# Seven block products for the second half of the output gate and for the retention branch's gate, with their sums on VectorE and the convolution constants loaded row by row

## The chip, the cores and the metric

The kernel runs on one core of one Trainium2 chip. The metric is the device time of one execution in microseconds (us), lower is better. The engines are called as the profile calls them: PE (TensorE, matmuls), PEld (its weight loads), DVE (VectorE), ACT (ScalarE), POOL (GpSimd), SP (SyncE, which here only issues DMAs). L12 is line 12 of the kernel before.

## The reference, cut to what matters

One layer of a hybrid backbone on 128 context and 512 latent tokens, 640 rows in all, model width 1024. The normalised and modulated input `h` goes through one wide projection `w_in`; attention and retention use slices of it:

```python
z = h @ w_in
q, k, v, rq, rk, rv, rg, ga, gr = jnp.split(z, np.cumsum(IN_SPLITS)[:-1].tolist(), axis=-1)
...
o = rms_scale(o_f + o_b[:, :, ::-1])
o = o.transpose(0, 2, 1, 3).reshape(B, L, RET_V)
yr = jax.nn.silu(rg.astype(jnp.float32)) * o
...
y = jax.nn.sigmoid(ga) * (ya @ w_att_o) + jax.nn.sigmoid(gr) * (yr @ w_ret_o)
return y @ w_out
```

`rg` (1024 columns) is the output gate of retention, `gr` (1024 columns) the gate of the retention branch. After this come a gated residual, a second norm, a gated MLP with a width-3 convolution (constants `conv_w`, `conv_b`), and a final norm.

## The kernel before

**Precision.** Each matmul operand is split into a high part (a cast to the matmul type) and a low part (the rest), and each product is three matmuls: high by high, high by low, low by high. A helper `w_split` (L139) makes the parts of a weight: the high part by ACT (L147), the low part by DVE (L152), or, with `"dma"`, by a negated copy on ACT and an accumulating DMA issued by POOL. Raw weights come by `w_raw` (L136) into two buffers of 8 KB per partition (tag `raw`); parts lie in eight buffers of 1024 columns (tag `wh`).

**Two forms of projection.** `a_group` keeps 128 tokens stationary and streams 512 weight columns: five banks, twelve matmuls of 512 columns for each half of the contraction and each token tile, 120 in all (L159 to L161). `b_col` keeps 128 weight columns stationary and streams 320 tokens: two banks of 24 matmuls (L197 to L199).

**Seven products.** The output projection `w_ret_o` (`ret_unit`, L1114) already uses Winograd's form of Strassen's scheme. A unit is 256 output columns; contraction, tokens and columns are each cut in two, and instead of eight block products it makes seven (numbered 1, 5, 6, 2, 3, 7, 4), each of twelve matmuls of 320 columns, on sums of blocks. The sums of the activations are made once by `ret_sums` (L1076, in tiles `ys`), those of the weights for each unit by `wsum` (L1129). `prod` (L1169) issues a product and takes its bank into the outputs; `prep` (L1133) makes the parts of one weight block; `ret_pump` (L1219) runs `prep` ahead of the products as far as the `wh` buffers go.

**Order around the change.** After the value projection (`rv1`) `states` (L909) makes the chunk states `Ss`. `retention` (L1011) runs ten groups (five token tiles by two halves of the heads) in three steps: `ret_a` (transposed keys `rkT`), `ret_b` (scores, L980, masked by DVE at L982) and `ret_c` (L989, L991; the square sums go to `sso`). The scaled queries `qd` (four buffers) are moved by `ret_q` (L955) on SP's queue and scaled at L969. `conv_load` (L1005) waits for the first `rkT` by a copy on POOL (L1006) and then issues four DMAs of single elements, three of `conv_w` (L1008) and one of `conv_b` (L1009). `ret_d` (L998) normalises a half of the heads; its root is a chain of thirteen small DVE steps and a scaling (`rsqrt`, L210 to L222), followed by five multiplications (L1003). Between these run the blocks of `rg0`, the first half of the output gate, by `a_group`; `evac_rg` (L1035) applies tanh (L1038) and multiplies (L1039, L1041). Then come the second half, `evac_rg(1)`, by `a_group`; then eight columns of the branch gate by `b_col` in `gr_col` (L1103; tanh at L1105), with the transposes of the gated retention output (`yr_blocks`, L1062 to L1067, parts by L665 and L666) and `ret_sums` beside them; then the four units of `w_ret_o`.

Outside the blocks marked `manual_schedule` a planner orders the instructions of every engine, and it may issue loads well ahead of their place in the program; inside such a block the named engines keep the written order. The block that holds the branch gate and `w_ret_o` fixes PE, DVE and ACT.

## Time and profile before

| | |
|---|---|
| median of three runs | 1138.04 us (1137.78 to 1138.88) |
| the profiled execution | 1138.44 us |
| its span, first to last instruction | 1136.7 us |
| mean granted PE clock | 0.998 |
| instructions | 17580 |

The span is what the profile's rows cover; the 1.7 us between it and the execution's time lie outside them. In the views that follow, a group's row has the line, the engine, the operation, output and inputs, the shape and the count, then busy time and the mean length of one in ns, then the idle time of the engine just before it and what ended that. A row of the timeline starts with the start time and the length in us, with the wait before it in brackets at its end.

### The profile page before, as it was taken

The page shows a single profiled execution, that of the slowest core. Times are in us where ns is not written, and L with a number is a line of the kernel's source. Part 1 is how long each engine was busy: PE and PEld are TensorE (multiplying, and loading weights), DVE is VectorE, ACT ScalarE, POOL GpSimd, SP SyncE. Part 2 cuts the span into 40 slices and gives each one's busy share as a digit, 9 for nine tenths or more (in the row PEclk, how much of TensorE's full clock was granted, in tenths as well). Part 3 has the DMA queues.
Part 4 walks back from the last instruction along what each step waited for, and adds up shares of the span by engine and source line. Part 5 has one row for each costly group of instructions (what it writes and reads, how often), then busy time and mean ns, then how long its engine had stood idle before and what let it go on. Part 6 is the DMA issues. An engine that isn't in the chain of part 4 may idle for free.

```text
span 1136.7 us, 17580 instructions
## 1 busy us (share of the span) xinstructions
PE 1109.3 (98%) x6757; PEld 1009.6 (89%) x6757; DVE 844.2 (74%) x1456; ACT 594.5 (52%) x1120; POOL 142.9 (13%) x171
## 2 busy tenths in 40 slices
PE   5999999999999999999999999999999999999996
PEld 4788899999989878889999889999899899899995
DVE  4667877669959947565857648968687598589888
ACT  5355756554244234534336436677557466475473
POOL 0042200000000010000003032012111111121012
PEclk9999999999999999999999999999999999999999
DMA  9742111016945734611228937456657646576552
GB/s 307 246 152 74 39 37 38 2 37 215 323 146 174 243 115 110 78 38 38 74 72 163 302 132 212 130 112 121 143 139 158 157 80 167 130 128 155 136 130 93
DMA packets 139316, 151.99 MB, mean 134 GB/s; under 512 B 27976, under 2 KB 108952, under 8 KB 138976
## 3 DMA queue, kind: packets, MB, share of 16 engines
q1 hardware_dynamic: 109856, 119.65, 33.3%
q0 software_dynamic: 29104, 31.10, 17.2%
q8 instruction: 53, 0.87, 0.3%
q14 instruction: 31, 0.25, 0.1%
q10 hardware_dynamic: 272, 0.11, 0.0%
HBM read 115.71 MB, written 8.67 MB: 109 GB/s over the span
## 4 chain that ended last, share of the span: by engine, by line
PE 88%; DVE 5%; ACT 3%; issue 2%; DMA 1%; SPq 0%; ACTq 0%; DVEq 0%; POOL 0%
DMA weights.raw.247_7726<-in_w_down 1%; DVE x1.u1.1_6330 L1496 1%; DMA ret2.qd.12_4681<-ret.u5.5_3422 0%; DMA const.u2.2_72<-in_b_mod 0%; DVE x1.u1.1_6330 L1545 0%; DVE x1.u1.1_6330 L1303 0%; PE mm3.mm.75_6171 L1176 0%; DVE acts.u2.2_91 L432 0%; PE mm1.mm.11_294 L161 0%; PE mm7.mm.59_10668 L1619 0%; PE mm7.mm.17_8071 L1619 0%; PE mm7.mm.41_9543 L1619 0%; PE mm7.mm.59_10668 L1618 0%; PE mm7.mm.44_9776 L1618 0%; PE mm7.mm.38_9294 L1619 0%
## 5 line engine op out<-in xcount | busy, mean ns | idle before, releaser
L1148 POOL DMA_DIRECT2D weights.wh.164_5865<-weights.raw.156_5798 x1 | 1.3, 1327 | 146.9 <-DVE f1.s.15_5209 L1187 146.9
L816 POOL DMA_DIRECT2D spill.u2.2_2891<-f1.s.1_1160 x1 | 0.6, 580 | 129.7 <-DVE mod.u3.3_2846 L604 129.7
L1633 DVE TENSOR_TENSOR t7.u4.4_6818<-t7.u4.4_6818,const.u1.1_70 128x320 f32<-128x320 f32 x10 | 4.9, 494 | 11.4 <-ACT const.u1.1_70 L1632 11.4
L152 DVE TENSOR_TENSOR weights.wh.113_4453<-weights.raw.111_4450,weights.wh.112_4452 128x1024 fp32r<-128x1024 f32 x1 | 1.2, 1227 | 13.1 <-ACT weights.wh.112_4452 L147 13.1
L938 DVE SCALAR_TENSOR_TENSOR ret2.u1.1_4263<-ret2.u1.1_4263,const.u11.11_86 64x128 f32<-64x128 f32 x24 | 6.8, 338 | 2.9 <-ACT ret2.u1.1_4263 L931 2.8
L940 DVE SCALAR_TENSOR_TENSOR ret2.u1.1_4263<-ret2.u1.1_4263,const.u11.11_86 64x128 f32<-64x128 f32 x24 | 6.6, 382 | 2.8 <-ACT ret2.u1.1_4263 L933 2.8
L429 ACT CAST acts.u1.1_90<-f0.s.2_104 128x640 fp32r<-128x640 f32 x4 | 2.9, 728 | 9.5 <-DVE f0.s.2_104 L427 9.5
L553 ACT ACTIVATE f0.s.3_710<-f0.s.3_710,p1q.ny20.11_878 128x128 f32<-128x128 f32 x20 | 6.0, 388 | 2.5 <-DVE p1q.ny20.11_878 L220 2.5
L446 PE MATMUL aux1.aux.1_134<-const.u1.1_70,const.u2.2_72 80*128 80x80 f32 x1 | 0.4, 367 | 7.1 <-DMA const.u2.2_72<-in_b_mod 7.1
L429 ACT CAST acts.u1.1_90<-f0.s.1_103 128x640 fp32r<-128x640 f32 x4 | 2.9, 727 | 8.3 <-DVE f0.s.1_103 L427 8.3
L299 POOL DMA_DIRECT2D mod.acc.24_3630<-in_b_mod x2 | 1.7, 858 | 42.5 <-ACT ret.u5.5_3422 L874 42.5
L147 ACT CAST weights.wh.67_3284<-weights.raw.66_3282 128x1024 fp32r<-128x1024 f32 x1 | 1.1, 1052 | 11.3 <-PE mm3.mm.8_3125 L198 11.3
L147 ACT CAST weights.wh.77_3520<-weights.raw.76_3518 128x1024 fp32r<-128x1024 f32 x1 | 1.0, 1048 | 11.2 <-PE mm3.mm.16_3382 L198 11.2
L584 POOL TENSOR_TENSOR p1.u1.1_604<-p1.u3.3_608,p1q.u1.1_598 128x512 f32<-128x512 f32 x1 | 1.3, 1302 | 44.5 <-DMA p1.u4.4_610<-in_cache_k 44.5
L1150 DVE TENSOR_TENSOR weights.wh.152_5717<-weights.raw.151_5663,weights.wh.152_5717 128x512 fp32r<-128x512 f32 x1 | 0.7, 693 | 8.3 <-ACT weights.wh.152_5717 L1141 8.3
L147 ACT CAST weights.wh.132_5219<-weights.raw.131_5217 128x1024 fp32r<-128x1024 f32 x1 | 1.1, 1055 | 11.0 <-PE mm3.mm.49_5037 L160 11.0
L1507 DVE TENSOR_TENSOR x1.u1.1_6330<-x1.u1.1_6330,gate.u1.1_6316 128x512 f32<-128x512 f32 x10 | 6.7, 693 | 0.0
L553 ACT ACTIVATE p1.u4.4_610<-p1.u4.4_610,p1.ny10.15_660 128x128 f32<-128x128 f32 x10 | 3.0, 389 | 6.5 <-DVE p1.ny10.15_660 L220 6.5
L1540 POOL TENSOR_TENSOR x1.u1.1_6330<-x1.u1.1_6330,weights.raw.422_10889 128x512 f32<-128x512 f32 x3 | 4.9, 1632 | 12.2 <-ACT x1.tm.111_10902 L1513 9.4
L446 PEld LDWEIGHTS aux1.aux.1_134<-const.u1.1_70,const.u2.2_72 80*128 80x128 f32 x1 | 0.2, 182 | 7.0 <-issue 7.0
L152 DVE TENSOR_TENSOR weights.wh.83_3656<-weights.raw.81_3653,weights.wh.82_3655 128x1024 fp32r<-128x1024 f32 x1 | 1.2, 1226 | 6.9 <-ACT weights.wh.82_3655 L147 6.9
L553 ACT ACTIVATE f0.s.4_959<-f0.s.4_959,p1q.ny20.20_1127 128x128 f32<-128x128 f32 x20 | 6.2, 396 | 0.0
(6808 smaller groups left out, 4938.1 us busy)
## 6 DMA issues: line engine op xcount, KB each, us to landing
spill.u1.1_2890<-x1.u1.1_6330 POOLq DMA_DIRECT2D x5, 512.0 KB, 3.9
xin.u1.1_102<-in_x_sample SPq DMA_DIRECT2D x4, 512.0 KB, 4.6
p0.u5.5_119<-in_w_mod SPq DMA_DIRECT2D x2, 1024.0 KB, 10.0
p0.u6.6_125<-in_w_mod SPq DMA_DIRECT2D x2, 1024.0 KB, 14.9
p0.u7.7_128<-in_w_mod SPq DMA_DIRECT2D x2, 1024.0 KB, 12.3
...
```

The source lines that it names most:

```text
L147: nc.scalar.copy(hi, rv)
L152: (lo_eng or V).tensor_sub(lo, rv, hi.bitcast(F32))
L299: nc.gpsimd.dma_start(accs[v][0:1, c, :], a["b_mod"][0:1, col:col + DM], accum_op=ALU.add)
L429: nc.scalar.copy(hT[0][:, k, :], xk)
L553: nc.scalar.activation(x[:, j], x[:, j], AF.Copy, scale=rstd[:, j:j + 1])
L584: nc.gpsimd.tensor_mul(ct, r2[:, :, 0, :], gqk[:, i:i + 1, :].to_broadcast([P, 4, P]))
L938: V.scalar_tensor_tensor(Ss[0:64, hh, st + 1, j], Ss[0:64, hh, st, j], cdsel[0:64, h:h + 1], Ss[0:64, hh, st + 1, j], op0=ALU.mult, op1=AL ...
L940: V.scalar_tensor_tensor(Ss[64:128, hh, 2 - st, j], Ss[64:128, hh, 3 - st, j], cdsel[64:128, h:h + 1], Ss[64:128, hh, 2 - st, j], op0=ALU. ...
L1496: V.tensor_add(x1[:, t, gs], x1[:, t, gs], down_mul(ps, t, c0))
L1507: V.tensor_mul(x1[:, t, gs], x1[:, t, gs], gb[:, t == 0, gs])
L1540: eng.tensor_mul(x, x, fg[:, c0:c0 + 512])
L1633: V.tensor_sub(his[1], his[1], u3[i])
```

## The change

Both gates are moved to the seven-product form, as six units of 256 columns ahead of the four units of `w_ret_o`, all in one list of products with one `ret_pump`.

- `h_sums` makes the four sums of blocks of `h` on DVE, in pieces of 640 columns, between the steps of `states` and of `retention`. Its running sum `x` borrows one of the two `raw` buffers; the fourth sum goes to the space of `Ss` for the first half of the heads and is made late.
- `in_unit` prepares weight blocks as `ret_unit` does, but the low parts of products 2, 3 and 7 go by accumulating DMA, and the high part of 7 by a copy on DVE. `rg_col` and `gr_col` apply tanh afterwards, in place, from SBUF.
- The low parts of `rg0` go by DMA.
- The second half of the heads is normalised, transposed and gated inside the list (`plan`): the transposes of that half are multiplied by the gate straight from PSUM, and the low parts and sums of the retention output are spread over the products.
- `ret_d` takes its root from one power on POOL and one refinement on DVE.
- `conv_load` loads one row at a time, at groups 2, 4, 6 and 8, each after a copy on POOL that waits for the keys of the group before.
- `r2k` has five buffers, not six; `r1` and `crow` lie in other pools; pool `f1` closes early and `hs` takes its place.

```diff
     def r2k():
-        return rp([P, 512], tag="r2k", bufs=6)
-
-    r1 = rp([P, NT, 2, 64])
+        return rp([P, 512], tag="r2k", bufs=5)
+
+    r1 = modp([P, NT, 2, 64])
...
+    def h_sums():
+        q = {m: [z.bitcast(F32) for z in hq[m]] for m in hq}
+        x = wp([P, 4 * 512], F32, tag="raw", bufs=2)[:, :4 * HALF].rearrange("p (k t) -> p k t", k=4)
...
+        yield from diff(x, q[1, 1], q[1, 0])
+        yield from low(1)
+        yield from neg_sum(x, q[0, 0])
+        yield from low(2)
+        yield from diff(h3, q[0, 0], q[1, 0])
+        yield "late"
+        yield from neg_sum(h4, q[0, 1])
...
     def ret_d(hh):
-        rso = rsqrt(rs2, sso[:, hh].rearrange("p t h -> p (t h)"), 4 * NT, 1.0 / P, post=0.5)
+        rso = sso[:, hh].rearrange("p t h -> p (t h)")
+        y = cv[:, 4:7, :].rearrange("p r c -> p (r c)")[:, :4 * NT]
+        V.tensor_scalar(rso, rso, 1.0 / P, EPS, op0=ALU.mult, op1=ALU.add)
+        nc.gpsimd.tensor_tensor(y, rso, cst[:, C_NH:C_NH + 1].to_broadcast([P, 4 * NT]), op=ALU.pow)
+        yield
+        V.tensor_mul(rso, rso, y)
+        V.tensor_mul(rso, rso, y)
+        V.tensor_scalar(rso, rso, -0.25, 0.75, op0=ALU.mult, op1=ALU.add)
+        V.tensor_mul(rso, rso, y)
...
-    def conv_load(after):
-        nc.gpsimd.tensor_copy(cw[:, :, 0], after)
-        for i in range(3):
-            nc.sync.dma_start(cw[:, i, :], a["conv_w"][0, i].rearrange("(c p) -> p c", p=P))
-        nc.sync.dma_start(cw[:, 3, :], a["conv_b"][0].rearrange("(c p) -> p c", p=P))
+    def conv_load(i, after):
+        nc.gpsimd.tensor_copy(cw[:, i, :1], after)
+        src = a["conv_w"][0, i] if i < 3 else a["conv_b"][0]
+        nc.sync.dma_start(cw[:, i, :], src.rearrange("(c p) -> p c", p=P))
...
-            if i == 1:
-                conv_load(sa[0][2][:, :4])
+            if i in (2, 4, 6, 8):
+                conv_load(i // 2 - 1, sa[i - 1][2][:, :1])
...
-    rg0 = a_group(w_in[:, O_RG:O_RG + 512], hTk, mm, evac_rg(0))
+    rg0 = a_group(w_in[:, O_RG:O_RG + 512], hTk, mm, evac_rg(0), "dma")
...
-    run(a_group(w_in[:, O_RG + 512:O_RG + 1024], hTk, mm, evac_rg(1)))
...
+        def prep(m):
+            low_part()
+            src = bs[SRC[m]]
+            hi, lo = halves_of(m, ops, src, V.tensor_copy if m == 7 else nc.scalar.copy)
+            if m in (2, 3, 7):
+                nc.scalar.activation(lo, src, AF.Copy, scale=-1.0)
+                nc.gpsimd.dma_start(lo, src, accum_op=ALU.add)
+            else:
+                low_later(bs, m, hi, lo, src)
...
+    units = [in_unit(O_RG + 512 + 2 * p * P, 4 + 2 * p, rg_col(4 + 2 * p)) for p in range(2)]
+    units += [in_unit(O_GR + 2 * p * P, 2 * p, gr_col(2 * p)) for p in range(4)]
...
+    order = [(1, 5, 2, 6, 3, 7, 4)] * (NU + NR)
+    wait = [2, 2, 4, 4, 4, 2] + [2] * NR
...
+    for i, _ in enumerate(retention()):
+        if i >= 16 or not hold:
+            hold = next(hsum, None) == "late"
+            if i >= 16:
+                next(hsum, None)
+        if i % 3 == 2:
+            next(rg0, None)
+        if i == 18:
+            ret_pump(-1, 0)
+    run(hsum)
+    ret_pump(-1, 4)
+    run(rg0)
+    ret_pump(0, 7)
...
+        def yr_block(g, t):
...
+            if g:
+                d = thr[:, 4:8, ts]
+                V.tensor_mul(d, d, p3)
+                return
...
-        for c in range(KD):
-            if c % 2 == 0 and c + 2 < KD:
-                graw = wgr(c + 2)
-            for _ in gr_col(c, wg):
...
-            if n == 15:
+            for n0, fn in plan:
+                if n0 == n:
+                    fn()
+            if n == 7 * NU + 15:
                 units[-1][3]()
-            ret_pump(n + 1, min(5 + n, 8))
+            ret_pump(n + 1, min(7 + n, 8))
```

More of the change, by code (lines that the diff above doesn't have):

```diff
@@ L103, in hybrid_step @@
     ident = cst[:, C_ID:C_ID + P]
-    crow = cp([80, P])
+    crow = xp([80, P])
     for i, n in enumerate(("c", "c_ctx", "norm1_g", "norm2_g")):
@@ L1198, in ret_unit, with halves_of @@
-        return load, prep, prod, reload
+                nc.scalar.copy(u(0)[:, his], ps)
+                later.extend(col(0))
+            else:
+                V.tensor_sub(u(1)[:, los], u(1)[:, los], ps)
+        return prod
+    def halves_of(m, ops, src, copy=nc.scalar.copy):
+        t_ = wp([P, 1024], F32R, tag="wh", bufs=8)
+        hi, lo = (t_[:, z * 512:(z + 1) * 512].rearrange("p (k n) -> p k n", n=P) for z in range(2))
+        copy(hi, src)
+        ops[m] = (hi, lo)
+        return hi, lo
@@ new lines, in rg_col, with f, fin, gr_col @@
+    def rg_col(t0):
+        def f(c):
+            def fin():
+                for ts in (los, his):
+                    th, x = aux([P, 512], tag="aux")[:, :HALF], thr[:, t0 + c, ts]
+                    nc.scalar.activation(th, x, AF.Tanh, scale=0.5)
+                    V.scalar_tensor_tensor(x, th, 1.0, x, op0=ALU.add, op1=ALU.mult)
+            return [(1, fin)]
+        return f
+    def gr_col(t0):
+        def f(c):
+            def fin():
+                x = thr[:, t0 + c, :]
+                nc.scalar.activation(x, x, AF.Tanh, scale=0.5)
+            return [(1, fin)]
+        return f
```

333 lines of the change are left out of this document (198 added, 135 removed).

## The prediction

> **What bounds the kernel now.** I read the page's totals and its chain first, then the windows of the stages that the diff touches, then what TensorE (PE) waited for.
>
> ```profile
> span 1136.7 us, 17580 instructions
> ...
> PE 1109.3 (98%) x6757; PEld 1009.6 (89%) x6757; DVE 844.2 (74%) x1456; ACT 594.5 (52%) x1120; POOL 142.9 (13%) x171
> ...
> PE 88%; DVE 5%; ACT 3%; issue 2%; DMA 1%; SPq 0%; ACTq 0%; DVEq 0%; POOL 0%
> ```
>
> ```profile
> 449.00:498.00 49.00, 47.68 (x333) 43.08 (x332) 32.51 (x66) 26.57 (x54) 0.24 (x1) 1.00 0.44 46
> ...
> 498.50:586.40 87.90, 87.90 (x546) 83.16 (x546) 55.33 (x71) 30.61 (x48) 0.00 (x0) 1.00 0.18 60
> ...
> 586.00:637.00 51.00, 50.81 (x343) 50.05 (x342) 35.55 (x56) 28.18 (x56) 12.99 (x12) 1.00 0.77 164
> ...
> 765.00:790.00 25.00, 25.00 (x172) 25.00 (x171) 23.48 (x41) 18.55 (x38) 5.10 (x4) 1.00 0.60 122
> ```
>
> ```profile
> PE aux3.aux.33_4802 L980 <- DVE ret.r2k.39_4752 L982: 1.3, 1, 1.3
> ...
> PE acc7.acc.11_7972 L159 <- ACT gt.gt0.11_7900 L1418: 1.0, 1, 1.0
> ```
>
> The windows give, after the stretch and its length, busy time of PE, PEld (weight loads), DVE, ACT and POOL, the granted clock, and the DMA share. Retention proper lies in 449 to 498; the second half of the output gate (evac_rg(1)) and the whole branch gate (gr_col) in 498.5 to 586.4; the seven-product projection w_ret_o in 586 to 637. In 498.5 to 586.4 PE has no gap at all, at clock 1.00, and neither DVE nor ACT is near it. So what counts there is the number of matmuls; a removed one is worth its issue interval as long as no other engine takes over. PE's only wait of size nearby is the 1.3 us at L980.
>
> **The change, part by part.** First the matmuls. A busy PE record overlaps its neighbour, so I take intervals between blocks of 12 matmuls.
>
> ```profile
> 515.13 0.60 ACT L1038 ACTIVATE ret.r2k.56_5130<-mm3.mm.45_5033 128x512 f32<-128x512 f32 x1 [1.89 <-PE mm3.mm.45_5033 L161]
> ...
> 517.85 0.60 ACT L1038 ACTIVATE ret.r2k.57_5146<-mm3.mm.46_5034 128x512 f32<-128x512 f32 x1 [2.12 <-PE mm3.mm.46_5034 L161]
> ...
> L197 PE MATMUL mm3.mm.53_5387<-acts.u1.1_90,weights.wh.132_5219 x4: 309/309/309, 540.7 to 542.0; 128*128 128x320 f32 x4
> ...
> L197 PE MATMUL mm3.mm.54_5424<-acts.u1.1_90,weights.wh.137_5353 x4: 309/309/309, 544.2 to 545.5; 128*128 128x320 f32 x4
> ...
> L1176 PEld LDWEIGHTS mm3.mm.66_5784<-yr.u1.1_5203,weights.wh.152_5717 x4: 188/188/188, 586.3 to 587.6; 128*128 128x128 f32 x4
> L1176 PE MATMUL mm3.mm.66_5784<-yr.u1.1_5203,weights.wh.152_5717 x4: 308/310/312, 586.5 to 587.8; 128*128 128x320 f32 x4
> ...
> L1176 PE MATMUL mm3.mm.66_5784<-rt.u2.2_5415,weights.wh.158_5802 x4: 309/309/309, 595.3 to 596.6; 128*128 128x320 f32 x4
> ```
>
> Twelve 512-column matmuls take 517.85 - 515.13 = 2.72 us. Twelve of 320 columns take (544.2 - 540.7)/2 = 1.75 in gr_col, and in the existing seven-product form, from product 1 (586.5) to product 7, five products later, (595.3 - 586.5)/5 = 1.76; I use 1.755. Output gate, second half: 120 matmuls of 512 are 10 x 2.72 = 27.2 us; two units of seven products are 14 x 1.755 = 24.6: -2.6. Branch gate: four pairs of columns of 8 blocks are 32 x 1.755 = 56.2; now 28 x 1.755 = 49.1: -7.1. Together **-9.7 us**; the 4.5 us left of the stage (87.9 - 83.4) are the 40 transposes of yr, as many after.
>
> [...]
>
> Now what takes the matmuls' place on DVE and ACT.
>
> ```profile
> 503.18 3.10 DVE L1003 TENSOR_TENSOR f0.s.6_3420<-f0.s.6_3420,ret2.ny20.28_5012 128x512 f32<-128x512 f32 x5
> ...
> 501.04 0.18 DVE L218 TENSOR_TENSOR ret2.nt20.29_5013<-ret2.ny20.28_5012 128x20 f32<-128x20 f32 x1
> ...
> 496.04 1.23 DVE L152 TENSOR_TENSOR weights.wh.130_5115<-weights.raw.126_5108,weights.wh.129_5114 128x1024 fp32r<-128x1024 f32 x1 [0.15 <-ACT weights.wh.129_5114 L147]
> ...
> 614.52 0.82 DVE L1167 TENSOR_TENSOR acts.u2.2_91<-f1.s.16_5210,acts.u1.1_90 128x640 fp32r<-128x640 f32 x1
> ...
> L1097 DVE TENSOR_TENSOR f0.s.7_5413<-rt.u1.1_5208,f0.s.7_5413 128x1280 fp32r<-128x1280 f32 x1 | 1.5, 1492 | 1.3 <-ACT f0.s.7_5413 L1096 1.3
> ...
> 597.59 0.48 DVE L1187 TENSOR_TENSOR f1.s.15_5209<-f1.s.15_5209,mm3.mm.68_5851 128x320 f32<-128x320 f32 x1
> ...
> L1334 DVE CAST acts.u1.1_90<-x1.row.30_6641 x1: 428/428/428, 684.8 to 684.8; 128x512 fp32r<-128x512 f32 x1
> ...
> 528.20 0.59 ACT L665 CAST yr.u1.1_5203<-aux3.aux.47_5244 128x512 fp32r<-128x512 f32 x1 [1.59 <-PE aux3.aux.47_5244 L1067]
> 528.68 0.59 ACT L665 CAST yr.u1.1_5203<-aux3.aux.48_5251 128x512 fp32r<-128x512 f32 x1
> ...
> L1141 ACT CAST weights.wh.153_5721<-weights.raw.151_5663 128x512 fp32r<-128x512 f32 x1 | 0.6, 622 | 1.5 <-DVE weights.raw.151_5663 L1131 1.5
> ...
> L1185 ACT ACTIVATE f1.s.16_5210<-mm3.mm.66_5784 128x320 f32<-128x320 f32 x1 | 0.4, 429 | 0.0
> ...
> L1096 ACT CAST f0.s.7_5413<-rt.u1.1_5208 128x1280 fp32r<-128x1280 f32 x1 | 1.3, 1262 | 1.4 <-DVE rt.u1.1_5208 L1087 1.4
> ```
>
> Five of L1003 fill 3.10 us though one lasts 0.69, so back to back they step by (3.10 - 0.69)/4 = 0.60: I take 0.09 off each DVE duration, and 0.1 off ACT's (0.59 against a step of 0.48). New stage length on PE: 42 x 1.755 + 4.5 = 78.2 us.
> DVE in it: a gate unit has 4 low parts and 4 weight sums (8 x 0.60), one copy (0.34) and 3 additions of 320 columns (3 x 0.39), 6.3; six are 38. Gate multiplies of evac_rg's successor 8 x 0.39 = 3.1, normalisation 3.7 (five of L1003 and four small steps), five products from PSUM 3.0, eleven passes of 1280 columns (low parts and sums) 11 x 1.40 = 15.4. Sum 63.2, or **81%**, against 55.33 of 87.9 before.
> ACT: per unit 6 high parts and 3 negated copies (0.52 each, taken alike), 5 evictions (0.33) and some 1.3 of tanh, 7.6; six are 45.6; about 13 copies of 512 columns 6.5, nine passes of 1280 at 1.16, 10.4. Sum 62.5, **80%**, against 30.61. In 765 to 790 the same seven-product form runs with DVE at 94% and ACT at 74%, and PE never waits; so I let the cover hold, with 0.5 us for small waits (PE loses 51.00 - 50.81 = 0.2 in the present w_ret_o stage).
>
> In front of this stage DVE gains the sums of h: 24 passes of 640 columns at 0.73, 17.5 us. It loses 8 low parts of 1024 (first gate half to DMA, second gone), 8 x 1.14 = 9.1, and about 16 small steps of the root at 0.18 (L218), 2.9. Its power of 20 columns on POOL has no row here: between 0 and, if DVE stands for it, the 13 steps (2.3) that it replaces; PE has blocks of rg0 meanwhile, so 0. That leaves +5.5 beside the 32.51 of 49 us: hidden under PE. The DMA low parts of the first half start about 421.2 and are wanted at 438.36:
>
> ```profile
> 419.01 1.05 ACT L147 CAST weights.wh.114_4456<-weights.raw.111_4450 128x1024 fp32r<-128x1024 f32 x1 [0.33 <-PE mm3.mm.39_4182 L160]
> ...
> 438.36 0.39 PE L160 MATMUL mm3.mm.40_4445<-weights.wh.113_4453,acts.u1.1_90 128*128 128x512 f32 x1
> ...
> 473.16 0.69 DVE L969 TENSOR_TENSOR ret2.qd.12_4681<-ret2.qd.12_4681,ret.u3.3_3418 128x512 f32<-128x512 f32 x1 [5.04 <-DMA ret2.qd.12_4681<-ret.u5.5_3422]
> ...
> 451.46 7.78 SPq L1008 DMA_DIRECT2D const.u14.14_89<-in_conv_w  x3
> 459.28 3.32 SPq L1009 DMA_DIRECT2D const.u14.14_89<-in_conv_b  x1
> 462.71 3.70 SPq L136 DMA_DIRECT2D weights.raw.131_5217<-in_w_in  x1
> 466.51 2.56 SPq L955 DMA_DIRECT2D ret2.qd.12_4681<-ret.u5.5_3422  x4
> ...
> 510.83 1.05 ACT L147 CAST weights.wh.132_5219<-weights.raw.131_5217 128x1024 fp32r<-128x1024 f32 x1 [10.99 <-PE mm3.mm.49_5037 L160]
> ...
> DMA to landing us min/median/max: 4.3/6.4/8.3
> ...
> DMA to landing us min/median/max: 4.9/5.2/8.8
> ```
>
> The last two rows are landing times of 256 KB accumulates (L1148) and 1 MB weight loads (L136). Twice the accumulate's median for 512 KB, 12.8, is early; twice 8.3 lands just then. Hidden: 0.
>
> **Constants row by row.** Now conv_load holds SyncE's queue from 451.46 to 462.6, qd.12 is issued at 466.51, DVE stands 5.04 us for it, and that is the L980 wait. Afterwards each row (up to 3.3 us of queue) waits for a GpSimd copy that waits for one rkT; the qd loads of later groups stand behind that wait, but two iterations (about 2 x 4.9 us, ten in 49) lie between rows and each qd needs 2.6. The stall should go: -1.3; bounds -1.3 and, if DVE is late there anyway, 0.
>
> **Entry into the gate units.** The sums borrow one of two raw buffers (x), and h4 may be written only after group 4 has read Ss. So the first unit's weights load late, and product 2's low part is an accumulating DMA. If the planner runs loads ahead, as it did with raw.131 (issued 462.71, cast 510.83), they are there in time: 0. If the sums end where the program puts them, in the ninth of ten groups, near 491 (449 + 8.6 x 4.9): + 5.2 load + 3 preparing + 6.4 landing = 505.6, wanted two products after 498.5, at 502.0: +3.6. I take +1.0, near the planner's side and the size of the acc7 wait, the one wait at the start of a group. The other edits (crow, r1, five r2k buffers) move memory and no path: 0.
>
> **Sum** against the profiled execution, 1138.44 us (span 1136.7 and 1.7 around it): -9.7 - 1.3 + 1.0 + 0.5 = -9.5, so 1128.9; the median of the three runs is 0.4 lower, so **1128.5**.
>
> **Rivals.** 1. *DVE and ACT become the bound.* Each orders its work and waits for the other's half; a low part of weights waits up to 0.7 for its cast, a 1280 pass 1.3 (L1097). For: both near 80%, ACT doubled. Against: 765 to 790. If 24 weight parts and 6 passes all wait, DVE needs 63.2 + 16.8 + 7.8 = 87.8, 9.6 over: 1138; half of it, 1133.3. It decides where waits pass 78.2 - 63.2 = 15 us.
>
> ```profile
> 607.75 0.69 DVE L1150 TENSOR_TENSOR weights.wh.171_5961<-weights.raw.160_5823,weights.wh.171_5961 128x512 fp32r<-128x512 f32 x1 [0.69 <-ACT weights.wh.171_5961 L1141]
> ...
> 599.35 1.58 POOL L1148 DMA_DIRECT2D weights.wh.165_5869<-weights.raw.156_5798  x1
> ```
>
> 2. *The entry waits in full*, 3.6 rather than 1.0: 1131.1. For: the shared buffer; against: the planner.
> 3. *Weight loads set PE's pace.* Loads before: 120 + 384 = 504; after 168 + 336 = 504. At 0.188 each nothing is saved: 1138. Against: twelve take 1.755, 0.146 each, so loads overlap one another here, and 512-column pairs take 0.227. [...]
> 4. *Slower: the two raw buffers turn too slowly.* The load of unit p+2 waits until unit p's seventh product has its accumulate landed. Cycle for two units: load 5.2, six preparations about 1.25 (7.5), issue 1.6, landing 6.4: 20.7 of 2 x 12.3 = 24.6. For: a third accumulate per unit on POOL; against: landings of 4.3 to 8.3 at a DMA share of 0.77. Four units turn so; all 9.5 us are eaten at 2.4 per unit, a cycle of 29.4, from landings of 15 us on. At 17 the cycle is 31.3, +3.35 x 4 = 13.4 us: 1141.9.
>
> [...]
>
> **How the numbers follow.** Forecast 0.65 (1126.5 to 1130.5); rival 1 0.12 (three quarters of it still faster); rival 2 0.14; rival 3 0.03; rival 4 0.06. No more than 0.2% (2.3 us) can be told from no change. Faster 0.65 + 0.09 + 0.14 = 0.88; within 0.03 + 0.03 = 0.06; slower 0.06. Range 1126.5 (no entry wait, no small waits, half a microsecond for rounding) to 1133.5 (rival 2 whole, rival 1 to its half): about 0.84.
>
> **What would show it.** Products every 1.755 us; no L980 wait; a gate stage of about 78 to 80 us with DVE and ACT near 80%; PE's wait list naming the first unit's wh.lo or nothing. PE waiting on low parts throughout is rival 1; on raw loads behind POOL accumulates, rival 4; products above 2.0 us with PE unbroken, rival 3.

## The result: no gain, 0.16% slower

The changed kernel takes 1140.14 us in the median of 20 runs (1137.69 to 1141.99), the kernel before 1138.09 us in as many beside them: ratio 1.0016, 95% interval 1.0009 to 1.0023. The forecast was 1128.5 us. The profiled execution took 1139.0 us, its span 1137.2. Its page, the totals and the shares of the chain that ended last:

```profile
PE 1102.2 (97%) x6757; PEld 1005.8 (88%) x6757; DVE 869.1 (76%) x1508; ACT 634.8 (56%) x1202; POOL 183.9 (16%) x201
...
PE 83%; DVE 6%; DMA 4%; ACT 3%; issue 2%; SPq 1%; POOL 0%; ACTq 0%; DVEq 0%; POOLq 0%
```

PE works 7.1 us less than before (1102.2 against 1109.3) and yet the span is 0.5 us longer: PE now stands 35.0 us of it, not 27.4. What it waits for between 400 and 640, by total, number and longest:

```profile
PE aux3.aux.13_4486 L971 <- ACT f0.s.6_3420 L852: 4.6, 1, 4.6
PE mm3.mm.57_5704 L1130 <- ACT rt.u1.1_5091 L1135: 1.9, 1, 1.9
PE aux3.aux.36_4870 L1031 <- DVE ret.r2k.41_4832 L1033: 1.5, 1, 1.5
PE aux3.aux.61_5518 L1353 <- DVE rt.u1.1_5091 L1208: 0.7, 1, 0.7
PE aux3.aux.42_4967 L1031 <- DVE ret.r2k.46_4918 L1033: 0.5, 1, 0.5
```

The first stand, 4.6 us before the second chunk state of the second half of the heads (L971), lies in front of retention, in a stretch that the prediction passed over. It costs more than it shows. Windows of 3.41 us around it (length, busy time of PE, PEld, DVE, ACT, POOL, granted clock, DMA share):

```profile
439.68:443.09 3.41, 0.59 (x3) 0.17 (x1) 3.38 (x13) 2.07 (x2) 0.00 (x0) 1.00 0.55 215
443.09:446.50 3.41, 1.62 (x7) 1.65 (x8) 3.40 (x10) 3.39 (x6) 1.68 (x3) 0.50 0.20 38
446.50:449.92 3.42, 3.42 (x11) 2.74 (x10) 3.42 (x8) 1.24 (x2) 1.46 (x2) 0.50 0.99 187
449.92:453.33 3.41, 3.41 (x24) 3.11 (x24) 2.20 (x6) 1.21 (x3) 0.00 (x0) 1.00 0.82 159
```

From 443.09 to 449.92 PE runs at half clock (the eight matmuls of L971 take 2.04 us there, 1.05 before the change): the 5.0 us of work in the second and third row would have taken 2.5, an estimate from that clock. So PE's busy time fell by 9.6 us through the matmuls, close to the 9.7 forecast, and rose by 2.5 through the clock, 7.1 in all; another 7.6 went into waiting. The rest of this document finds where those 10 us, 2.5 and 7.6, come from.

Why is L971 late? DVE's timeline ahead of it (start, length, wait before it in brackets), then the SyncE queue's and ACT's, and last the matching rows of the kernel before (the loads of qd.4, their scaling and the keys):

```profile
431.84 0.69 DVE L1020 TENSOR_TENSOR ret2.qd.4_4574<-ret2.qd.4_4574,ret.u2.2_3418 128x512 f32<-128x512 f32 x1 [4.62 <-DMA ret2.qd.4_4574<-ret.u4.4_3422]
...
434.10 1.55 DVE L939 SCALAR_TENSOR_TENSOR weights.raw.116_4492<-weights.raw.116_4492,acts.u1.1_90 128x640 f32<-128x640 f32 x2
...
437.45 0.81 DVE L941 TENSOR_TENSOR weights.raw.116_4492<-weights.raw.116_4492,acts.u2.2_91 128x640 f32<-128x640 f32 x1
...
439.07 0.82 DVE L941 TENSOR_TENSOR weights.raw.116_4492<-weights.raw.116_4492,acts.u2.2_91 128x640 f32<-128x640 f32 x1
439.92 3.31 DVE L990 SCALAR_TENSOR_TENSOR ret2.u1.1_4272<-ret2.u1.1_4272,const.u10.10_86 64x128 f32<-64x128 f32 x12
443.24 0.83 DVE L948 TENSOR_TENSOR hs.b.4_4267<-weights.raw.116_4492,hs.b.3_4266 128x640 fp32r<-128x640 f32 x1
443.99 0.75 DVE L968 TENSOR_TENSOR ret.r2k.26_4483<-ret.u3.3_3421,const.u11.11_87 128x256 f32<-128x256 f32 x2
```

```profile
421.17 5.14 SPq L1006 DMA_DIRECT2D ret2.qd.4_4574<-ret.u4.4_3422  x4
...
436.94 0.49 SPq L136 DMA_DIRECT2D weights.raw.117_4725<-in_w_in  x1
```

```profile
439.92 1.26 ACT L945 CAST hs.b.3_4266<-weights.raw.116_4492 128x1280 fp32r<-128x1280 f32 x1 [5.41 <-DVE weights.raw.116_4492 L941]
442.28 1.04 ACT L147 CAST weights.wh.118_4727<-weights.raw.117_4725 128x1024 fp32r<-128x1024 f32 x1 [1.10 <-DMA weights.raw.117_4725<-in_w_in]
...
444.31 0.59 ACT L852 COPY f0.s.6_3420<-mm3.mm.39_4182 128x512 f32<-128x512 f32 x1
```

```profile
421.95 2.61 SPq L955 DMA_DIRECT2D ret2.qd.4_4558<-ret.u5.5_3422  x4
...
426.04 0.69 DVE L969 TENSOR_TENSOR ret2.qd.4_4558<-ret2.qd.4_4558,ret.u3.3_3418 128x512 f32<-128x512 f32 x1 [0.33 <-DMA ret2.qd.4_4558<-ret.u5.5_3422]
...
438.63 0.76 DVE L918 TENSOR_TENSOR ret.r2k.27_4472<-ret.u4.4_3421,const.u12.12_87 128x256 f32<-128x256 f32 x2
```

The keys for L971 are made at L968, at 443.99; before the change at 438.63. DVE works in the planner's order here, and two things stand in it. It waits 4.62 us for the queries qd.4, whose four loads take 5.14 us of queue instead of 2.61: the accumulating DMAs of the output gate's low parts (issued at 419.17 and 422.04) are under way beside them, and the DMA engines are full (DMA share 1.09 from 421.17 to 426.31, each packet counted where it starts; 0.75 there before the change). And the second sum of h (L939, L941, L948) runs here, ahead of L990 and L968. ACT has a third candidate: its cast of that sum waits 5.41 us for DVE, then its cast of the gate's second raw block for a load issued at 436.94 (before: 405.63, when `x` did not hold that buffer); only then comes L852, the copy that the list of waits names. It ends at 444.90, the keys at 444.74, so the two chains end almost together.

### The profile page after: what moved, and what is told of

It is laid out like the page before. It is cut to its first block, busy times and chain, and to the rows that moved or that the text cites. A ratio compares the mean times of both kernels' runs of the same rounds, so it can differ in the third digit from the quotient of the medians.

```text
span 1137.2 us, 17834 instructions
## 1 busy us (share of the span) xinstructions
PE 1102.2 (97%) x6757; PEld 1005.8 (88%) x6757; DVE 869.1 (76%) x1508; ACT 634.8 (56%) x1202; POOL 183.9 (16%) x201
## 4 chain that ended last, share of the span: by engine, by line
PE 83%; DVE 6%; DMA 4%; ACT 3%; issue 2%; SPq 1%; POOL 0%; ACTq 0%; DVEq 0%; POOLq 0%
DMA weights.raw.156_5576<-in_w_in 1%; DMA weights.wh.153_5524<-weights.raw.140_5244 1%; DMA ret2.qd.4_4574<-ret.u4.4_3422 1%; SPq L1006 1%; DVE x1.u1.1_6516 L1661 1%; DMA weights.raw.266_7912<-in_w_down 1%; DMA weights.raw.117_4725<-in_w_in 0%; DMA xin.u1.1_72<-in_b_mod 0%; POOL const.u2.2_78 L1053 0%; DVE x1.u1.1_6516 L1710 0%; DVE x1.u1.1_6516 L1468 0%; PE mm3.mm.72_6356 L1130 0%; DVE acts.u2.2_91 L432 0%; PE mm1.mm.11_294 L161 0%; PE mm7.mm.8_7723 L1784 0%
## 5 line engine op out<-in xcount | busy, mean ns | idle before, releaser
L1053 POOL TENSOR_TENSOR const.u2.2_78<-const.u12.12_88,const.u1.1_70 128x20 f32<-128x20 f32 x2 | 7.1, 3552 | 4.7 <-DVE const.u12.12_88 L1052 4.7
L988 DVE SCALAR_TENSOR_TENSOR ret2.u1.1_4272<-ret2.u1.1_4272,const.u10.10_86 64x128 f32<-64x128 f32 x24 | 6.8, 338 | 1.3 <-ACT ret2.u1.1_4272 L981 1.2
L553 ACT ACTIVATE f0.s.3_710<-f0.s.3_710,p1q.ny20.11_878 128x128 f32<-128x128 f32 x20 | 6.0, 388 | 2.5 <-DVE p1q.ny20.11_878 L220 2.5
L990 DVE SCALAR_TENSOR_TENSOR ret2.u1.1_4272<-ret2.u1.1_4272,const.u10.10_86 64x128 f32<-64x128 f32 x24 | 6.6, 381 | 0.8 <-ACT ret2.u1.1_4272 L983 0.7
L968 DVE TENSOR_TENSOR ret.r2k.23_4394<-ret.u3.3_3421,const.u11.11_87 128x256 f32<-128x256 f32 x2 | 0.8, 422 | 8.0 <-PE aux3.aux.7_4294 L971 8.0
L971 PE MATMUL aux3.aux.13_4486<-f0.s.6_3420,ret.r2k.26_4483 128*128 128x128 f32 x8 | 2.0, 437 | 4.6 <-ACT f0.s.6_3420 L852 4.6
L971 PEld LDWEIGHTS aux3.aux.13_4486<-f0.s.6_3420,ret.r2k.26_4483 128*128 128x128 f32 x8 | 1.8, 327 | 5.0 <-ACT weights.wh.119_4728 L149 5.0
```

Source lines behind the costliest of these rows:

```text
L553: nc.scalar.activation(x[:, j], x[:, j], AF.Copy, scale=rstd[:, j:j + 1])
L971: nc.tensor.matmul(ps[:, j * P:(j + 1) * P], kvl[:, j].rearrange("p c d -> p (c d)"), rvv[hh][:, j, t, :], start=True, stop=True)
L988: V.scalar_tensor_tensor(Ss[0:64, hh, st + 1, j], Ss[0:64, hh, st, j], cdsel[0:64, h:h + 1], Ss[0:64, hh, st + 1, j], op0=ALU.mult, op1=AL ...
L990: V.scalar_tensor_tensor(Ss[64:128, hh, 2 - st, j], Ss[64:128, hh, 3 - st, j], cdsel[64:128, h:h + 1], Ss[64:128, hh, 2 - st, j], op0=ALU. ...
L1053: nc.gpsimd.tensor_tensor(y, rso, cst[:, C_NH:C_NH + 1].to_broadcast([P, 4 * NT]), op=ALU.pow)
```

## The experiments

Every kernel is the changed kernel with the edit shown, but for before_rows. Lines inserted shift the numbers: the scores' mask, L1033 in the changed kernel, is L1034 or L1036 in some. The planner orders each kernel anew, so what an edit is worth includes the order that follows from it. The table gives the ratio to the kernel before with its 95% interval, the median, and, from the profiled execution, PE's stands of at least 1 us between 400 and 640 and the 3.41 us stretches at half clock there. That execution is not always near the median: old_root's took 1142.09 us, c_h4's 1132.99 and c_root_k's 1130.80.

| run | ratio | median us | stands of PE, us | half-clock stretches |
|---|---|---|---|---|
| the changed kernel | 1.0016 (1.0009 to 1.0023) | 1140.14 | 4.6, 1.9, 1.5 | 2 |
| rg0_dve | 1.0017 (1.0006 to 1.0027) | 1139.25 | 3.1, 2.2, 1.5 | 3 |
| x_in_h3 | 1.0001 (0.9992 to 1.0009) | 1137.33 | 2.5, 1.9, 1.6 | 2 |
| p7_dve | 0.9998 (0.9990 to 1.0007) | 1136.85 | 5.0, 1.5 | 2 |
| before_rows | 0.9996 (0.9987 to 1.0004) | 1136.74 | none | 0 |
| sums_behind | 1.0019 (1.0008 to 1.0029) | 1139.51 | 2.7, 2.2, 2.1 | 2 |
| sums_behind_rg0 | 1.0016 (1.0007 to 1.0025) | 1139.06 | 3.1, 2.0, 1.9 | 2 |
| h4_late | 1.0039 (1.0027 to 1.0052) | 1142.25 | 4.3, 2.7, 2.1 | 3 |
| all3 | 0.9992 (0.9983 to 1.0001) | 1136.67 | 3.0, 1.9 | 2 |
| old_root | 1.0019 (1.0010 to 1.0028) | 1139.54 | 4.4, 2.7, 1.5 | 3 |
| c_root_k | 0.9952 (0.9940 to 0.9965) | 1132.13 | 1.5 | 0 |
| c_root_s | 0.9947 (0.9935 to 0.9960) | 1130.95 | 1.4 | 0 |
| c_root_s1 | 0.9945 (0.9932 to 0.9957) | 1130.61 | 1.6 | 0 |
| lo_pow | 0.9989 (0.9980 to 0.9998) | 1136.18 | 5.2 | 2 |
| lo_dma | 0.9984 (0.9975 to 0.9993) | 1135.00 | 3.2, 1.3 | 1 |
| lo_sums | 0.9959 (0.9947 to 0.9971) | 1132.56 | 2.6, 1.5 | 0 |
| lo_p7 | 0.9961 (0.9948 to 0.9974) | 1132.56 | 1.8, 1.7 | 1 |
| c_h4 | 0.9953 (0.9939 to 0.9966) | 1131.34 | 2.4 | 1 |

### One edit at a time

**rg0_dve**

```diff
-    rg0 = a_group(w_in[:, O_RG:O_RG + 512], hTk, mm, evac_rg(0), "dma")
+    rg0 = a_group(w_in[:, O_RG:O_RG + 512], hTk, mm, evac_rg(0))
```

> The changed kernel with one edit: the low parts of the first half of the output gate are made by DVE again and not by accumulating DMA. What is to be explained is PE's stand of 4.6 us before the chunk state of the second half of the heads (L971, 440.3 to 444.9) and the half clock behind it (about 2.5 us more). Theory A: the two accumulates of 512 KB share the DMA engines with the loads of qd, so that qd.4 lands at 431.8 instead of 426.0, DVE stands 4.6 us for it with the keys for L971 queued behind, and they keep the raw buffer until they have landed. Then here the qd loads take 2.6 us each again, raw.117 is issued some 10 us earlier, the gap is under 1 us, the clock stays at 1.00, and the time is 6 to 7 us below the changed kernel, about 1133.5. Theory B: the borrowed raw buffer alone is the cause; raw.117 still stands behind the qd loads, ACT waits for it ahead of L852, at least 3 us of the gap stay and the time is above 1137. Theory C: DVE is short of time for the sums; it now has 4 more low parts (4.6 us), the gap grows and the time is above 1141.

The time did not move. The qd loads do take 2.6 us again, but PE still stands 3.1 us before L971. In this run's waits the cause has another name than in the changed kernel (DVE, not ACT), and DVE's timeline shows it:

```profile
PE aux3.aux.13_4484 L971 <- DVE ret.r2k.26_4481 L968: 3.1, 1, 3.1
```

```profile
435.38 0.82 DVE L941 TENSOR_TENSOR weights.raw.116_4490<-weights.raw.116_4490,acts.u2.2_91 128x640 f32<-128x640 f32 x1
437.59 0.83 DVE L948 TENSOR_TENSOR hs.b.4_4267<-weights.raw.116_4490,hs.b.3_4266 128x640 fp32r<-128x640 f32 x1 [1.40 <-ACT hs.b.3_4266 L945]
438.45 3.31 DVE L990 SCALAR_TENSOR_TENSOR ret2.u1.1_4272<-ret2.u1.1_4272,const.u10.10_86 64x128 f32<-64x128 f32 x12
441.77 0.76 DVE L968 TENSOR_TENSOR ret.r2k.26_4481<-ret.u3.3_3421,const.u11.11_87 128x256 f32<-128x256 f32 x2
```

One pass of x, 1.40 us waiting for ACT's cast and one low part, 3.0 us, stand ahead of L990. Theories A and C each hold a part. Two other stands got a half-clock stretch that they did not have in the changed kernel (mean clock 0.83 in 480 to 490 and in 560 to 570, 1.00 in the changed kernel), and that took back what the shorter stand gave.

**x_in_h3**

```diff
-        x = wp([P, 4 * 512], F32, tag="raw", bufs=2)[:, :4 * HALF].rearrange(...)
+        x = h3
...
-        yield from diff(h3, q[0, 0], q[1, 0])
         yield "late"
         yield from neg_sum(h4, q[0, 1])
+        yield from diff(h3, q[0, 0], q[1, 0])
```

> The changed kernel with one edit: the running sum x of h_sums lies in the space of the third sum h3 and not in a raw buffer, and h3 is made last, after the fourth sum. So both raw buffers serve the output gate, and its second raw block can be loaded some 30 us earlier, as before the change; the accumulating DMAs stay. Theory B (the borrowed buffer, with ACT standing in L147 for raw.117 and L852 queued behind it): the stand before L971 falls under 1.5 us, the clock stays at 1.00, and the time is 5 to 7 us below the changed kernel, about 1134. Theory A (the accumulates delay qd.4 and DVE): DVE still stands over 4 us for qd.4, at least 3 us of the stand stay, and the time is within 2 us of the changed kernel's 1140. Theory C (DVE is short of time): the stand stays and wait moves to the end of retention, where the sums of h3 now lie; above 1141.

Between the theories: raw block two is loaded at 404.48, ACT no longer stands for it, and 2.5 us of the stand stay, on DVE's L968. The gain of some 0.15% also contains a changed order of DVE, so what the borrowed buffer costs by itself is not separated.

**p7_dve**

```diff
-            hi, lo = halves_of(m, ops, src, V.tensor_copy if m == 7 else nc.scalar.copy)
-            if m in (2, 3, 7):
+            hi, lo = halves_of(m, ops, src, nc.scalar.copy)
+            if m in (2, 3):
```

> The changed kernel with one edit: in the gate units the parts of product 7 are made by ACT (high) and DVE (low), as in w_ret_o, so that a unit has two accumulating DMAs and not three. Rival 4 of the prediction, in the small: the third accumulate of unit 2 landed 9.1 us after its issue (545.95), raw.156 was issued only then (555.7), landed at 565.5, and PE stood 1.9 us for the first product of unit 4. If the third accumulate is what keeps the raw buffer, raw.156 is issued about 5 us earlier, the 1.9 us go, and the time falls by 1.5 to 2.5 us, to about 1138. If the accumulate of product 3, issued 1.8 us ahead of it, lands at nearly the same time, the wait stays above 1 us and the time within 0.7 us of 1140. If the extra DVE pass (0.6 us in each of six units) is what counts, it is slower.

The first outcome: the stand at mm.57 is gone and the ratio falls by 0.0018. In the changed kernel POOL, the queue and ACT show the chain: the third accumulate, which lands 9.5 us after its issue (the median of such accumulates is 4.7), the load that waits for the raw block it holds, and the cast that waits for the load:

```profile
545.95 1.73 POOL L1194 DMA_DIRECT2D weights.wh.153_5524<-weights.raw.140_5244  x1
```

```profile
555.69 0.37 SPq L136 DMA_DIRECT2D weights.raw.156_5576<-in_w_in  x1
```

```profile
565.80 0.62 ACT L1157 CAST weights.wh.162_5700<-weights.raw.156_5576 128x512 fp32r<-128x512 f32 x1 [4.62 <-DMA weights.raw.156_5576<-in_w_in]
```

**before_rows**: the kernel before, with `conv_load(i, after)` and its call at groups 2, 4, 6 and 8 as in the change's diff.

> The kernel before with one edit: the convolution constants are loaded row by row, as in the change. The prediction took 1.3 us off for it, the stand of PE at L980. If that step is right by itself and only something else in the change put a new wait in its place, the time is 0.8 to 1.5 us below the kernel before (ratio 0.9987 to 0.9993) and PE has no wait of over 0.5 us in retention. If the single rows stand in front of the qd loads just as the four did (in the changed kernel two of them went out together and held the queue for 9.2 us), the wait stays, at 0.8 us or more, and the ratio is 1.000 within its interval.

```profile
PE aux3.aux.39_4897 L980 <- DVE ret.r2k.44_4853 L982: 0.5, 1, 0.5
PE aux3.aux.42_4942 L980 <- DVE ret.r2k.47_4896 L982: 0.2, 1, 0.2
```

In the trace the wait of 1.3 us becomes 0.5 and 0.2. The ratio's interval allows a gain of 1.3 us and none; 0.5 us is its middle.

**old_root**

```diff
-        V.tensor_scalar(rso, rso, 1.0 / P, EPS, op0=ALU.mult, op1=ALU.add)
-        nc.gpsimd.tensor_tensor(y, rso, cst[...].to_broadcast([P, 4 * NT]), op=ALU.pow)
+        rso = rsqrt(..., sso[:, hh].rearrange("p t h -> p (t h)"), 4 * NT, 1.0 / P, post=0.5)
         yield
-        V.tensor_mul(rso, rso, y)
-        V.tensor_mul(rso, rso, y)
-        V.tensor_scalar(rso, rso, -0.25, 0.75, op0=ALU.mult, op1=ALU.add)
-        V.tensor_mul(rso, rso, y)
```

> The changed kernel with one edit: the root in ret_d is worked out by DVE's thirteen small steps again, and not by the power of 20 columns on POOL. In the changed kernel POOL takes 3.55 us for it and DVE, in its fixed order, stands 3.3 to 3.7 us for the result (487.6 to 491.3), with the masks of groups 6 and 7 (L1033) queued behind it; in the last runs that became PE's largest stand (3.0 us at the scores of group 8, and a half-clock window) as soon as the stands ahead of it were gone. Theory P (the power is in DVE's path and the prediction's zero for it was wrong): here DVE has no gap of over 1 us between 484 and 492, PE's wait of 0.5 us at group 8 goes, and the rest stays as in the changed kernel, since the larger stands are elsewhere: time 0 to 1.5 us below 1140. If DVE stands there for something else (the load of qd.16 or qd.18), the gap stays at over 2 us and the time is the same.

The wait of 0.5 us goes, but DVE then stands 2.19 us for a qd load in the same place, and the time is that of the changed kernel: by itself the edit gains nothing.

**h4_late**

```diff
+                if i == 8:
+                    V.tensor_scalar(neg1, sb[7][:, 0, :1], 0.0, -1.0, op0=ALU.mult, op1=ALU.add)
...
-        yield from neg_sum(h4, q[0, 1])
+        yield from neg_sum(h4, q[0, 1], neg1[:, :1])
```

Here `neg_sum` takes its factor -1 from a value that DVE makes of a chosen tile, so that the planner cannot put the sum ahead of that tile.

> The changed kernel with one edit: the fourth sum of h may start only when the scores of group 7 are masked (its factor -1 comes from them). In the changed kernel its four passes and the low part, 4.5 us, stand in DVE's order between 475.6 and 483.9, ahead of the mask of group 5 (L1033, 484.4), for which PE stands 1.5 us at L1031. If these passes are the cause of that wait, it falls under 0.5 us, no wait of over 0.7 us takes its place up to 510, and the time falls by 1 to 1.5 us, to about 1139. If the late load of qd.12 (DVE stands 2.1 us for it at 473) is the cause, the wait stays above 1 us and the time is the same. If the fourth sum is wanted earlier than it then comes, a wait appears at the third or fifth product of the first unit, and the time is above 1141.

```profile
479.42 0.81 DVE L939 SCALAR_TENSOR_TENSOR ret2.u1.1_4272<-weights.raw.116_4492,acts.u1.1_90 128x640 f32<-128x640 f32 x1
480.27 0.82 DVE L941 TENSOR_TENSOR ret2.u1.1_4272<-ret2.u1.1_4272,acts.u2.2_91 128x640 f32<-128x640 f32 x1
...
482.42 1.49 DVE L1330 TENSOR_TENSOR acts.u2.2_91<-ret2.u1.1_4272,acts.u1.1_90 128x1280 fp32r<-128x1280 f32 x1
...
484.43 0.69 DVE L1033 TENSOR_TENSOR ret.r2k.41_4832<-aux3.aux.33_4833,ret.u1.1_3417 128x512 f32<-128x512 f32 x1
```

These are the rows of the changed kernel that the edit moves. The stand of 1.5 us goes, as said, but one of 2.7 us appears at group 8 with a half-clock stretch: a miss, and by the ratios some 2.6 us slower.

### Two causes at once

**sums_behind**: the same means, for the second sum.

```diff
+                if hh and t == NT - 1:
+                    V.tensor_scalar(neg1[:, :1], kvl[:, 0, 0, :1], 0.0, -1.0, op0=ALU.mult, op1=ALU.add)
```

> The changed kernel with one edit: the sums of h after the first one may not start before the last keys of the chunk states (L968) are made; the factor -1 of neg_sum is taken from a value that DVE works out of those keys. So four passes of x, the cast of the second sum and its low part leave DVE's order ahead of L990 and L968. The accumulating DMAs of the output gate stay. Theory D (both causes add up in DVE's order: the late qd.4 gives about 5.8 us, the sums ahead of L990 about 3.1, and 1.7 of slack is to be used up first): the stand before L971 falls from 4.6 to about 2.5 us, one half-clock window of 3.4 us instead of two, and the time falls by 3 to 4 us, to about 1136.5. Theory A (the accumulates alone): the stand stays above 4 us, within 1 us of 1140. Theory C (the sums alone): the stand goes under 0.5 us, the clock stays at 1.00, 1133.5.

**sums_behind_rg0**: this edit and that of rg0_dve.

> Both edits together: the later sums of h stand behind the keys of the chunk states, and the low parts of the first half of the output gate are made by DVE. The run with the second edit alone still had a stand of 3.1 us, and ahead of L990 there DVE made one pass of x (0.8), stood 1.4 us for ACT's cast of the second sum and made its low part (0.8): 3.0 us. Theory D (both causes add up): nothing is left of the stand (under 0.5 us), no half-clock window before 480, and the time is 5.5 to 7 us below the changed kernel, about 1134. If a third cause holds L971 (the order of ACT, with L852 behind the casts of the output gate), over 2 us of the stand stay and the time is above 1137.

Alone the edit leaves 2.7 us of the stand, as theory D has it; together nothing is left, though `x` still holds its raw buffer. So the borrowed buffer does not make the stand by itself. ACT's order, which these edits change too, was not held apart from DVE's. The times do not follow, since two new stands come, in the combined run:

```profile
PE aux3.aux.42_4965 L1034 <- DVE ret.r2k.46_4916 L1036: 3.1, 1, 3.1
PE mm3.mm.57_5702 L1133 <- ACT rt.u1.1_5089 L1138: 2.0, 1, 2.0
PE aux3.aux.19_4607 L1034 <- ACT ret2.rkT.6_4589 L1025: 1.9, 1, 1.9
```

**all3**: these two, p7_dve and h4_late.

> All edits together: low parts of the first half of the output gate by DVE, the later sums behind the keys of the chunk states, the fourth sum behind the mask of group 7, and product 7 of the gate units with its parts by ACT and DVE. If the four stands of PE in the changed kernel (4.6 with its half clock 2.5, 1.5, 0.5, 1.9) are all that ate the gain of the products, and each edit takes its own away, the time is 9 to 10 us below the changed kernel's 1140 and 7 to 9 below the kernel before: ratio 0.992 to 0.994. If DVE is short of time (these edits give it about 5 us of low parts back and squeeze the sums into a shorter stretch), new waits on DVE appear between 450 and 500 and the ratio is above 0.996.

The gain of 9 us does not come: 0.9992. Both new stands are there. One is ACT's order, where the cast of the second sum waits for DVE with the next keys' copy behind it; the other is DVE's, where the power on POOL is waited for (a wait of 3.90 us for the load of qd.16 lies just ahead of it). ACT's rows of all3, then DVE's, where the wait for the power is the same in the changed kernel (3.68 us), and last the power's own row in the changed kernel's list of groups:

```profile
449.88 1.26 ACT L946 CAST hs.b.3_4266<-weights.raw.116_4491 128x1280 fp32r<-128x1280 f32 x1 [3.22 <-DVE weights.raw.116_4491 L942]
...
451.77 0.37 ACT L1025 COPY ret2.rkT.6_4589<-aux3.aux.17_4584 128x256 f32<-128x256 f32 x1
```

```profile
484.00 0.17 DVE L1055 TENSOR_SCALAR const.u12.12_88<-const.u12.12_88 128x20 f32<-128x20 f32 x1
487.86 0.18 DVE L1058 TENSOR_TENSOR const.u12.12_88<-const.u12.12_88,const.u2.2_78 128x20 f32<-128x20 f32 x1 [3.69 <-POOL const.u2.2_78 L1056]
```

```profile
L1053 POOL TENSOR_TENSOR const.u2.2_78<-const.u12.12_88,const.u1.1_70 128x20 f32<-128x20 f32 x2 | 7.1, 3552 | 4.7 <-DVE const.u12.12_88 L1052 4.7
```

### All four causes, and each one put back

c_root_k is rg0_dve, sums_behind, p7_dve and old_root. c_root_s ties the second sum to the mask of group 0 instead; c_root_s1 also gives the gate's second raw block back to DMA.

> The changed kernel with the low parts of the first half of the output gate by DVE, the second sum of h behind the keys of the chunk states, product 7 of the gate units by ACT and DVE, and the old root on DVE; the fourth sum of h stays where the change has it. The run with the first three of these (and a late fourth sum) had stands of 3.0 us at the scores of group 8 and 1.9 us at those of group 0, each with a half-clock window. Theory P (DVE's stand for the power makes the first of these): it falls under 1 us, its half-clock window goes, and the time is about 4 to 5 us below that run's 1136.7, about 1132.5, ratio 0.9955 to 0.9965. If the late qd loads make it, over 2 us of the stand stay and the ratio is 0.998 to 1.000.

> As the run before it in this list, with one difference: the second sum of h may start only when the scores of group 0 are masked, and not at the end of the chunk states. In the run with all edits ACT's cast of the second sum stood 3.2 us for DVE (to 449.9) with the copy of the next keys (rkT.6, 451.8) queued behind it, and PE stood 1.9 us at the scores of group 0. If that order on ACT is the cause, the stand and its half-clock window go (3.6 us), and the time is 2.5 to 4 us below the run before it in this list, about 1129, ratio 0.992 to 0.994, unless the sums, now squeezed into retention with some 45 of 50 us on DVE, make a new wait of over 1 us at a mask (then the ratio is above 0.995).

> As the run before it in this list, but only the first raw block of the output gate's first half has its low parts by DVE; those of the second block go by accumulating DMA, as in the change. That takes 2.3 us off DVE between 440 and 450 and puts 1 MB of accumulates at 444 to 455, where no load of qd is under way. If DVE's load is what is left of the waits in retention, the time is 0.5 to 1.5 us below the run before it in this list. If accumulates anywhere near retention are the harm, a wait for qd or for the raw block of the first gate unit appears and it is 1 us or more above it.

c_root_k came out as theory P says, 1132.1. It differs from all3 in the fourth sum too, so the power's own price is that of lo_pow below. The step to c_root_s is smaller than expected (0.0005 in the ratio, inside the intervals): the stand at group 0 goes, one of 1.4 at the outputs of group 6 comes (aux.40, for the copy of the outputs of group 5, which the last expectation below counts as group 6). DMA low parts for the second block show no harm. c_root_s1 is the fastest, 0.55% (0.43 to 0.68) under the kernel before:

```profile
PE 1100.3 (97%) x6757; PEld 1004.4 (89%) x6757; DVE 874.6 (77%) x1529; ACT 632.9 (56%) x1200; POOL 164.5 (15%) x191
```

```profile
PE aux3.aux.40_4939 L1041 <- ACT f0.s.6_3420 L1047: 1.6, 1, 1.6
PE aux3.aux.61_5537 L1351 <- DVE rt.u1.1_5116 L1206: 0.7, 1, 0.7
PE aux3.aux.36_4885 L1032 <- DVE ret.r2k.41_4832 L1034: 0.7, 1, 0.7
```

With the four stands cleared, each edit was taken back out of c_root_s1 alone.

> The version with all four edits (c_root_s1, 1130.6, no half-clock window, PE's largest stand 1.6 us), with one taken back: the root of ret_d is a power on POOL again. Theory P: DVE stands some 3.7 us for it in front of the masks of groups 6 and 7, PE stands 2 to 3 us at the scores of group 8 and gets a half-clock window (1.7 us more); less what the 13 small steps save, 3 to 4.5 us slower, 1134 to 1135. If there is slack for it now, within 0.7 us of 1130.6.

> The version with all four edits, with one taken back: the low parts of the first raw block of the output gate go by accumulating DMA again. Theory A: the loads of qd.4 and qd.5 take about 5 us instead of 2.6, DVE stands over 4 us for qd.4, and with 1.7 us of slack before L971 PE stands 2 to 3 us there and gets a half-clock window: 3.5 to 4.5 us slower, about 1134.5. If only the sums ahead of the keys mattered, within 0.7 us of 1130.6.

> The version with all four edits, with one taken back: the second sum of h is free to run ahead of the keys of the chunk states again. Theory C: three microseconds of DVE stand ahead of L990, as in the run with the low parts by DVE alone, where PE stood 3.1 us before L971 and got a half-clock window: 3.5 to 5 us slower, about 1134.5 to 1135.5, less up to 1.4 us if the stand of 1.6 us that the later sums make at the end of retention goes. If only the accumulates mattered, within 0.7 us of 1130.6.

> The version with all four edits, with one taken back: the low part of product 7 goes by a third accumulating DMA in each gate unit again, and its high part by DVE. In the changed kernel that made a stand of 1.9 us at the first product of unit 4, with or without a half-clock window from run to run: 2 to 3.7 us slower, 1132.5 to 1134.5. If the raw block comes in time now that all units start earlier against nothing else, within 0.5 us of 1130.6.

PE's longest stand in lo_pow, then in lo_dma:

```profile
PE aux3.aux.40_4928 L1041 <- ACT f0.s.6_3420 L1047: 5.2, 1, 5.2
```

```profile
PE aux3.aux.13_4487 L972 <- DVE ret.r2k.26_4484 L969: 3.2, 1, 3.2
```

By differences of the ratios to c_root_s1's 0.9945, times 1137: the power on POOL costs 5.0 us, the accumulates of the first raw block 4.4, the second sum ahead of the keys 1.6, the third accumulate 1.8, each to about 2. So the first two are clear of noise and the last two are not: for these speak the stands that come back in their traces (2.6 us before the chunk state in lo_sums, 1.8 at mm.57 in lo_p7), and for the third accumulate also p7_dve. The four add up to 12.8, while all together are worth 8.1 (1.0016 against 0.9945): in the changed kernel they partly hide one another, as rg0_dve and old_root show, which gained nothing by themselves. lo_pow's stand came at the outputs of group 6 and not, as expected, at the scores of group 8. lo_sums was dearer in the forecast, since its stand of 2.6 us was expected to bring a half-clock stretch and did not.

**c_h4**: c_root_s1 and h4_late's edit.

> The version with all four edits, and the fourth sum of h behind the mask of group 7, the edit that made the changed kernel 2 us slower by itself. In the version with all four edits ACT's cast of the fourth sum stands 3.6 us for DVE with the squares and the copy of group 6 (L1046, L1047) queued behind it, and PE stands 1.6 us for that copy. If that is the cause, this stand goes, and if the loss of the edit by itself came only from the power on POOL, nothing takes its place: 1 to 2 us below 1130.6, about 1129.2. If the fourth sum is late there by itself, a stand of over 1 us appears at the third product of the first unit or at the last groups, and the time is 1130.5 or more.

A miss: the stand of 1.6 us goes, and one of 2.4 comes where product 7 of the first gate unit wants a copy of ACT (L1139). By their times in the trace, ACT makes it behind the cast of a weight sum (507.93) that DVE ends only at 507.86, since the fourth sum's low part (499.93) and the small steps of the root (to 504.05) stand ahead of it. The time is that of c_root_s1 within the intervals: the fourth sum needs its time somewhere, and moving it gains nothing.

## Why the prediction was wrong, step by step

The term for the matmuls was right. The sum failed at three terms that it put at nothing (the accumulating low parts, the sums of h, the power on POOL) and at the 0.5 us for small waits in the gate stage; none of them asked what is queued behind.

- **Matmul savings, -9.7: right.** Products of twelve matmuls follow each other every 1.76 us (584.50, 586.26, 588.02 in the changed kernel), and PE's time fell by 9.6 with the clock taken out, by 9.0 to 9.5 in the four runs that have no half-clock stretch before the last matmul (c_root_k, c_root_s, c_root_s1, lo_sums). So rival 3 is out: with as many weight loads in the gate stage as before (546 in the windows of both), PE is busy there for 79.0 us instead of 87.9.
- **The gate stage, 78.2 us with DVE at 81% and ACT at 80%: right but for its waits.** From its first product to the first of w_ret_o, changed kernel and c_root_s1:

```profile
506.38:588.02 81.64, 79.01 (x547) 78.28 (x546) 66.44 (x107) 62.47 (x119) 26.55 (x19) 1.00 0.86 155
```

```profile
499.11:578.90 79.79, 78.81 (x548) 78.29 (x546) 68.87 (x117) 62.49 (x119) 16.16 (x13) 1.00 0.69 139
```

  DVE is at 81% and ACT at 77% of the first row; rival 1 did not come. Its small waits were 2.6 us, not 0.5: 0.7 at a transpose that waits for a gate multiply of DVE (L1353) and 1.9 for rival 4's mechanism, in one place rather than four.
- **"Hidden: 0" for the low parts of the first half: the step that failed first.** It asked when the low parts are wanted, and not which loads are under way beside the transfers. The qd loads were late, in front of a DVE that keeps its order: 4.4 us (lo_dma).
- **Sums of h, "+5.5 beside the 32.51 of 49 us: hidden": failed.** The average over retention was right and the place wrong: the planner put the second sum ahead of the chunk states' keys, where DVE had 1.5 us of slack (before the change keys done at 439.4, PE at them at 440.9). That made a stand of 3.1 us in rg0_dve and of 2.6 in lo_sums, where the time rose by 1.6, not clear of noise.
- **The power on POOL, "so 0": failed, and with the low parts the dearest.** The upper bound, 2.3, let DVE stand no longer than the 13 steps that the power replaces. In the changed kernel's rows it takes 3.55 us and DVE stands 3.68 for it; with what DVE has queued behind, and half clock, 5.0 us (lo_pow).
- **Constants row by row, -1.3: half or less.** The prediction put two iterations between rows, but the first two went out together and held SyncE's queue for 9.20 us (from 458.19), so that qd.12 was still late: DVE waits 2.06 us for it in the changed kernel and 3.6 in before_rows, after 5.04 before. In before_rows 0.7 us of PE's wait stays. In the changed kernel the wait that replaced it (1.5) is the fourth sum's.
- **Entry, +1.0: nothing of it came.** The planner loaded the first unit's block at 453.45; c_root_s1 has 0.3 us there.
- **The half clock was in no term.** A stand was priced at its length; the first one, 4.6 us long, cost 7.1.
- The other edits (five `r2k` buffers, `r1` and `crow` elsewhere) were not tried by themselves.

The rival on the slower side (rival 4) had a real mechanism at a wrong place and size. Most of the forecast's sum comes true once the four waits are cleared: c_root_s1 is 6.2 us under the kernel before (4.9 to 7.7), of 9.5 forecast. Of the 3.3 missing, its trace shows stands of 1.6 and 0.7 in retention, where the forecast left none, and 1.1 in the gate stage (79.8 against 78.7), less the entry's 1.0; what is left lies within the interval.
